# Scores of an attention layer from two fp16 parts instead of two fp32r parts, with the norm weights of queries and keys evened out by a power of two

## The chip, the core and the metric

One core of one Trainium2 chip runs the whole kernel in one launch. The metric is device time in microseconds (us): the median of several executions. A profiled execution of the same program gives the trace; its time is named beside the others, since sums over rows belong to it. The engines are called as in the trace: PE is TensorE, PEld its weight loads, DVE VectorE, ACT ScalarE, POOL GpSimd, SP the engine that issues most DMAs.

## The reference, cut to what matters

An encoder of two layers over 256 positions of width 1024, in fp32. Each layer has a mixer and a channel part. In the mixer 16 heads of width 64 fall into three groups: "a" (4 heads, neighbourhood attention with a bias), "d" (6 heads, dilated windows, partial rotation), "c" (6 query heads on 2 key heads, axial rotation).

```
qa = rms_norm(heads(qa, H_NA), qg[0]);  ka = rms_norm(heads(ka, H_NA), kg[0])
qd = partial_rotary(rms_norm(heads(qd, H_DIL), qg[1]), cos1, sin1)      # kd likewise with kg[1]
qc = axial_rotary(rms_norm(heads(qc, H_GQ), qg[2]), cos_r, sin_r, cos_c, sin_c)   # kc with kg[2]
s = einsum(q, k) * hd ** -0.5 (+ bias or mask);  p = softmax(s);  o = p @ v
x = x + concat(rms_norm of each group's o) @ w_out
```

The norm weights qg and kg have 64 entries for each layer and group; here they are around 4 rather than 1. A score depends on the product of the query's and the key's weights alone, so one number may be moved from the one to the other. The channel part is `x + (gelu(conv(h @ w_g)) * (h @ w_u)) @ w_dn` with 2816 columns in each half.

## The kernel before

All large products are made of two parts for each operand, a high part and the rest, in three matmuls (high by high, high by rest, rest by high). For projections, output projection and the down projection the parts are fp32r; ACT casts the weights from the loaded tile `raw` to `hi`, and DVE subtracts to get `lo` (`split`, lines 638 and 639). Later steps of the channel part use fp16 parts, and so do the products of softmax and values (`weigh`, lines 1204 to 1225). The scores (`scores`, lines 1167 to 1188) use fp32r parts of queries and keys.

The 16 heads of a layer are worked in 8 pairs. For a pair, `scores` issues one burst of 12 matmuls: two query tiles of 128, three products, two heads. The two heads of a pair lie in partitions 0 to 63 and 64 to 127, so each matmul has 64 rows of weights by 128 columns (the queries) and moves 256 columns (the keys). `weigh` issues a burst of 12 as well, with 128 rows by 64 columns of weights (the values) and 256 moved columns of fp16 (the softmax). Between bursts PE is given pieces of the projections and of the output projection (`Weave`), so that it has work while DVE, ACT and POOL do softmax.

Queries and keys are made in `normed` (squares on ACT into a scratch tile of the tag `s2k`, sums, `rstd_of` on POOL with a power of -1/2, then the scaling of the projection into `z`), then in `rotated` (DVE, with tables made by POOL from the norm weights in `tables_d` and `tables_c`), then transposed by PE, and in `transposed` (lines 985 to 994) ACT copies the high part out of PSUM and DVE subtracts to get the rest. For group "a" there is no rotation: `tables_a` multiplies both norm weights into one tile `gna` of 64 columns, and `prep_a` multiplies the query half of `z` by it. In layer 0 the tables are made when the norm weights `gq` and `gk` have landed (they are issued on SP behind the first weights); those of layer 1 are made in the channel part of layer 0.

Nothing is written in its final order. Each call is recorded with a cost in ns (`cost`, lines 396 to 432; `together` gives a burst one cost for all), and `order` (lines 322 to 386) picks again and again the operation that can start first by these costs; at equal times the one that comes first in the program (`rank`). Each engine then works its queue strictly in that order. Tiles of one tag are handed out strictly in program order: an operation whose tile is not next in turn can't be picked (line 352, in which `s.given` is the number handed out so far):

```
                        if t.turn != s.given + n or len(s.free) <= n:
                            at = None
                            break
```

So a change of costs or of the operations that take a tag's tiles can change the order on every engine.

Of the kernel before, what the change touches and what calls it, by code (L numbers as in the profile page):

```python
# [11 lines left out]
F32 = mybir.dt.float32  # L12
F32R = mybir.dt.float32r
F16 = mybir.dt.float16
BF16 = mybir.dt.bfloat16
I32 = mybir.dt.int32
AF = mybir.ActivationFunctionType
ALU = mybir.AluOpType
AX = mybir.AxisListType

P = 128
S = 256
# [3 lines left out]
HD = 64  # L26
H_NA, H_DIL, H_GQ, H_GKV = 4, 6, 6, 2
# [4 lines left out]
DEPTH = 2  # L32
# [8 lines left out]
NS2K = 5  # L41
# [4 lines left out]
LIFT, TOP, TINY = 2.0**-30, 0x7F800000, 1e-30  # L46
# [181 lines left out]
class Plan:  # L228
# [5 lines left out]
    def pool(self, real, name, bufs, space=bass.MemoryType.SB):  # L234
        return PlanPool(self, real, name, bufs, space)
# [200 lines left out]
def encoder_kernel(  # L436
# [21 lines left out]
    nc = Plan(tc)  # L458
# [3 lines left out]
    const = pool("const", 1)  # L462
    wp = pool("wp", 3)
    act = pool("act", 2)
    small = pool("small", 4)
# [4 lines left out]
    def bcast_rows(row, n):  # L470
        return bass.AP(tensor=row.tensor, offset=row.offset, ap=[[0, P], [1, n]])
# [16 lines left out]
    def gains_T(i, n):  # L488
        w = 16 * n
        ps = psw.tile([P, 512], F32, tag="w", name=f"gps{i}")  # L490
        nc.tensor.transpose(ps[:, :w], gl0 if i == 0 else gl1, ident[:w, :w])
        for a in range(n):
            o, v = gains[:, i + a].rearrange("p l k -> p (l k)"), ps[:, 16 * a : 16 * a + 16]
            if i + a == 1:
                nc.vector.tensor_copy(o, v)
            else:
                nc.vector.tensor_scalar_mul(o, v, D**0.5)
# [287 lines left out]

    norms, tables, copied = {}, {}, {}

    def tables_d(l, which):
        g = norms[which]
        cd = act.tile([P, NT, HD], F32, tag=f"cd{which}", name=f"cd{which}{l}", bufs=1)  # L790
        sd = act.tile([P, NT, 16], F32, tag=f"sd{which}", name=f"sd{which}{l}", bufs=1)
        b = lambda v: v.unsqueeze(1).to_broadcast([P, NT, v.shape[1]])
        rot = norms["rot"]
        nc.gpsimd.tensor_tensor(cd, rot[:, :, 0:64], b(g[:, l, 1]), op=ALU.mult)
        for i in range(2):
            o, n = (8 * i, 8 * (1 - i)), 8
            nc.gpsimd.tensor_tensor(
                sd[:, :, o[0] : o[0] + n],
                rot[:, :, 64 + o[0] : 64 + o[0] + n],
                b(g[:, l, 1, o[1] : o[1] + n]),  # L800
                op=ALU.mult,
            )
        tables["d" + which, l] = cd, sd
# [16 lines left out]
        tables["c" + which, l] = cc, sc  # L820

    def tables_a(l):
        gna = act.tile([P, HD], F32, tag="gna", name=f"gna{l}", bufs=1)
        nc.gpsimd.tensor_tensor(gna, norms["q"][:, l, 0], norms["k"][:, l, 0], op=ALU.mult)
        tables["a", l] = gna

    load(0)
    for l in range(DEPTH):
# [79 lines left out]
        if l == 0:  # L908
            gains_T(1, 2)
            rot = const.tile([P, NT, 208], F32, tag="rot", name="rot")  # L910
            nc.sync.dma_start(rot, c_rot.rearrange("(t p) c -> p t c", p=P))
            gq = const.tile([P, DEPTH * 3 * HD], F32, tag="gq", name="gq")
            nc.sync.dma_start(gq, bcast_rows(q_norm_g, DEPTH * 3 * HD))
            gk = const.tile([P, DEPTH * 3 * HD], F32, tag="gk", name="gk")
            nc.sync.dma_start(gk, bcast_rows(k_norm_g, DEPTH * 3 * HD))
            dil = const.tile([P, NT, S], F32, tag="dil", name="dil")
            na_mask = const.tile([P, GRID_W], F32, tag="na", name="na_mask")
            na_repeat(0)
            norms["rot"] = rot
            norms["q"] = gq.rearrange("p (l a d) -> p l a d", l=DEPTH, d=HD)  # L920
            norms["k"] = gk.rearrange("p (l a d) -> p l a d", l=DEPTH, d=HD)

# [62 lines left out]
        def transposed(srcs, both, t, name):  # L985

            n = len(srcs)
            ps = psw.tile([P, 512], F32, tag="w", name=f"tr_{name}")
            for i, src in enumerate(srcs):
                nc.tensor.transpose(ps[:, i * P : (i + 1) * P], src, ident)  # L990
            pv = ps[:, : n * P].rearrange("p (k q) -> p k q", q=P)
            h, o = (z[:, :, t * P : (t + 1) * P] for z in both)
            nc.scalar.copy(h, pv)
            nc.vector.tensor_tensor(o, pv, h.bitcast(F32), op=ALU.subtract)

        def paired(which, group, n, zs, first=0):

            c = which + ("c" if group == "c" else "o")
            both = [act.tile([P, 3, S], F32R, tag=f"{c}{i}", name=f"{which}{i}{group}{l}", bufs=1)[:, :n] for i in range(2)]
            for t in range(NT):  # L1000
                transposed(pairs(zs[t], first, n), both, t, f"{which}{group}{l}{t}")
            return both
# [142 lines left out]
        def prep_a():  # L1145
            if l == 0:
                with nc.behind(hold["prep"]):
                    tables_a(l)
            gna = tables["a", l]
            for t in range(NT):  # L1150
                nm = f"a{l}{t}"
                z = normed(pj["aqk"][t], 2 * H_NA, t, nm)
                nc.vector.tensor_tensor(
                    z[:, 0:4], z[:, 0:4], gna.unsqueeze(1).to_broadcast([P, 4, HD]), op=ALU.mult
                )
                hold["a", t] = z

# [9 lines left out]
        def scores(i):  # L1167

            two = heads[i : i + 2]
            group = two[0].group  # L1170
            qs, ks = turned[group + "q"], turned[group + "k"]
            sps = [psw.tile([P, NT, S], F32, tag="w", name=f"s_{h.name}") for h in two]
            with nc.together(910):
                for t in range(NT):
                    c = slice(t * P, (t + 1) * P)
                    for n, (x, y) in enumerate(((0, 0), (0, 1), (1, 0))):
                        for h, rows_, sp in zip(two, (LOW, HIGH), sps):
                            nc.tensor.matmul(
                                sp[:, t], qs[x][rows_, h.h // 2, c], ks[y][rows_, h.kv if group == "c" else h.h // 2],
                                start=n == 0, stop=n == 2,  # L1180
                            )
            rs = small.tile([P, 2, NT], F32, tag="rs", name=f"rs_{two[0].name}")
            for a, (h, sp) in enumerate(zip(two, sps)):
                h.softens(sp, rs[:, a])
            nc.vector.reciprocal(rs, rs)
            wide = hold["rs", i] = act.tile([P, NT, 2, HD], F32, tag="re", name=f"re_{two[0].name}", bufs=2)
            for t in range(NT):
                nc.gpsimd.tensor_copy(wide[:, t], rs[:, :, t : t + 1].to_broadcast([P, 2, HD]))
# [367 lines left out]
```

## Time and profile before

| | us |
|---|---|
| median of 3 runs | 607.07 (606.72 to 607.68) |
| the profiled execution's own time | 610.95 |
| its span, first to last instruction | 609.2 |
| PE busy in it | 597.3 |
| DVE busy | 489.7 |
| ACT busy | 469.3 |
| POOL busy | 127.2 |
| mean granted clock of TensorE | 0.997 of full |

Busy is the time in which at least one instruction of the engine was under way. PE's matmuls are pipelined and their ends are modelled, so what a matmul costs is read from the distance of one start to the next. All lines of the kernel show as L393, the line that emits them; tiles tell them apart: `psw_w<-act_ko,act_qo` and `psw_w<-act_kc,act_qc` are scores, `psw_w<-act_ph,const_v` and `act_pl,const_v` are `weigh`, `wp_hi` and `wp_lo` are the parts of the weights.

### The profile page before, as it was taken

What the parts mean: (1) busy time and instruction counts of PE and PEld (TensorE: products, weight loads), DVE (VectorE), ACT (ScalarE), POOL (GpSimd) and SP (SyncE); (2) the same over time, 40 slices, a digit from 0 to 9 for tenths busy, and PEclk for the clock granted to TensorE, in tenths of its full rate; (3) what the DMA queues carried; (4) which work ended last, traced back from release to release, by engine and by line L of the source; (5) the groups of instructions that cost most, each with busy time, mean ns of one, the idle gap of its engine ahead of it and who ended that gap; (6) DMA issues with size and microseconds to landing.
All of it is one profiled execution on the core that took longest, in us unless ns stands there. A gap on an engine that the chain in (4) does not pass through costs nothing.

```text
span 609.2 us, 11253 instructions
## 1 busy us (share of the span) xinstructions
PE 597.3 (98%) x4092; PEld 509.0 (84%) x4092; DVE 489.7 (80%) x1095; ACT 469.3 (77%) x1060; POOL 127.2 (21%) x184
## 2 busy tenths in 40 slices
PE   9989999999999999999999999999999999999997
PEld 7879787788887888888889988877888888888886
DVE  5678999989996677867666899998899767777683
ACT  7677879697987778886378979887889897778750
POOL 0543242220021111341014223331101111111100
PEclk9989999999999999999999999999999999999999
DMA  8777222465576946565517721225655766656301
GB/s 292 227 228 216 95 88 80 145 226 190 164 209 221 265 148 220 187 207 190 156 52 225 253 90 69 76 80 200 208 185 178 260 208 208 207 186 211 125 33 70
DMA packets 85260, 104.75 MB, mean 172 GB/s; under 512 B 13044, under 2 KB 73044, under 8 KB 85204
## 3 DMA queue, kind: packets, MB, share of 16 engines
q1 hardware_dynamic: 84100, 103.31, 52.4%
q10 hardware_dynamic: 1104, 0.72, 0.4%
q8 instruction: 32, 0.52, 0.3%
q14 instruction: 24, 0.20, 0.1%
HBM read 102.98 MB, written 1.49 MB: 171 GB/s over the span
## 4 chain that ended last, share of the span: by engine, by line
PE 60%; DVE 16%; ACT 13%; DMA 4%; issue 3%; POOL 3%; ACTq 0%; DVEq 0%; POOLq 0%; SPq 0%
PE psa_a L393 31%; PE psw_w L393 28%; DVE wp_lo L393 5%; DVE act_s2k L393 4%; ACT wp_hi L393 3%; DVE wp_nl L393 3%; ACT act_s2k L393 3%; DMA wp_raw<-in_w_gate_up_dram 3%; ACT act_sw L393 3%; ACT wp_nh L393 2%; DMA wp_raw<-in_w_down_dram 2%; ACT act_hT L393 1%; POOL small_rstd L393 1%; POOL small_pw L393 1%; DVE act_cl L393 1%
## 5 line engine op out<-in xcount | busy, mean ns | idle before, releaser
L393 DVE TENSOR_TENSOR wp_lo<-wp_raw,wp_hi 128x512 fp32r<-128x512 f32 (+2 forms) x220 | 160.3, 756 | 18.3 <-ACT wp_hi L393 17.7
L393 PE MATMUL psw_w<-act_z,wp_nh 128*128 128x256 f16 x1024 | 169.3, 273 | 0.0
L393 ACT CAST wp_hi<-wp_raw 128x512 fp32r<-128x512 f32 (+2 forms) x220 | 138.3, 685 | 18.4 <-DMA wp_raw<-in_w_down_dram 8.6
L393 PE MATMUL psw_w<-act_z,wp_nl 128*128 128x256 f16 x512 | 139.3, 273 | 1.7 <-DVE wp_nl L393 1.6
L393 PE MATMUL psa_a<-wp_hi,act_hT 128*128 128x384 f32 (+2 forms) x448 | 116.2, 338 | 1.7 <-ACT wp_hi L393 1.6
L393 PEld LDWEIGHTS <-wp_nh 128*128 128x128 f16 x1024 | 98.1, 98 | 14.3 <-issue 1.7
L393 DVE SCALAR_TENSOR_TENSOR wp_nl<-wp_raw,small_pw,wp_nh 128x1024 f16<-128x1024 f32 x64 | 81.8, 1282 | 27.6 <-PE psw_w L393 21.0
L393 POOL TENSOR_TENSOR small_pw<-small_m,const_mh 128x1 f32<-128x1 f32 x40 | 41.6, 1042 | 275.9 <-DVE small_m L393 234.2
L393 ACT ACTIVATE wp_nh<-wp_raw,small_pw 128x1024 f16<-128x1024 f32 x64 | 71.4, 1141 | 17.1 <-DVE small_pw L393 13.2
L393 PEld LDWEIGHTS psa_a<-wp_hi,act_hT 128*128 128x128 f32 x448 | 79.1, 191 | 5.5 <-ACT wp_hi L393 2.2
L393 PE MATMUL psa_a<-wp_lo,act_hT 128*128 128x384 f32 (+2 forms) x224 | 76.1, 340 | 2.1 <-DVE wp_lo L393 1.9
L393 ACT ACTIVATE act_sw<-wp_raw 128x1024 f16<-128x1024 f32 x64 | 67.2, 1051 | 7.6 <-DMA wp_raw<-in_w_gate_up_dram 6.8
L393 PE MATMUL psa_a<-wp_hi,act_ch 128*128 128x512 f32 (+1 forms) x176 | 70.5, 402 | 0.5 <-ACT act_ch L393 0.5
L393 PE MATMUL psa_a<-wp_lo,act_ch 128*128 128x512 f32 (+1 forms) x176 | 69.3, 395 | 0.0
L393 PE MATMUL psa_a<-wp_hi,act_cl 128*128 128x512 f32 (+1 forms) x176 | 69.1, 394 | 0.1
L393 PE MATMUL psw_w<-act_hT,wp_hi 128*128 128x512 f32 x192 | 67.7, 396 | 0.0
L393 PEld LDWEIGHTS <-wp_nl 128*128 128x128 f16 x512 | 50.1, 98 | 9.3 <-DVE wp_nl L393 3.6
L393 PE MATMUL psw_w<-act_hT,wp_lo 128*128 128x256 f32 x192 | 53.5, 282 | 0.2 <-DVE wp_lo L393 0.2
L393 PEld LDWEIGHTS psa_a<-wp_lo,act_hT 128*128 128x128 f32 x224 | 42.8, 191 | 5.2 <-DVE wp_lo L393 3.9
L393 PEld LDWEIGHTS psw_w<-act_hT,wp_hi 128*128 128x128 f32 x192 | 35.9, 188 | 7.8
L393 PEld LDWEIGHTS psa_a<-wp_hi,act_ch 128*128 128x128 f32 x176 | 33.2, 189 | 8.1 <-ACT act_ch L393 1.0
L393 PEld LDWEIGHTS psa_a<-wp_hi,act_cl 128*128 128x128 f32 x176 | 33.2, 188 | 8.1 <-DVE act_cl L393 0.5
(154 smaller groups left out, 1013.4 us busy)
## 6 DMA issues: line engine op xcount, KB each, us to landing
wp_raw<-in_w_gate_up_dram SPq DMA_DIRECT2D x44, 1024.0 KB, 5.0
wp_raw<-in_w_down_dram SPq DMA_DIRECT2D x22, 1024.0 KB, 5.5
wp_raw<-in_w_in_dram SPq DMA_DIRECT2D x14, 768.0 KB, 8.2
wp_raw<-in_w_in_dram SPq DMA_DIRECT2D x8, 1024.0 KB, 7.0
wp_raw<-in_w_out_dram SPq DMA_DIRECT2D x8, 768.0 KB, 4.2
wp_raw<-in_w_out_dram SPq DMA_DIRECT2D x4, 512.0 KB, 3.4
act_nab<-dram_scr SPq DMA_DIRECT2D x4, 448.0 KB
wp_raw<-in_w_in_dram SPq DMA_DIRECT2D x4, 192.0 KB, 5.0
```

The lines of the kernel that those rows point to most:

```text
L393: getattr(engine.real, method)(*map(real, args), **{k: real(v) for k, v in kw.items()})
```

## The change

Queries and keys are kept as fp16 parts. So that they fit fp16's range, a new function `balanced` moves a power of two from the keys' norm weights to the queries' or back, for each layer and group, once at the start of layer 0; for group "a" the queries and keys are each multiplied by their own norm weights rather than the queries by both. The cost that the planner is given for a burst of scores goes from 910 to 780. The three products, their number and their shapes stay.

```
+    def balanced(gq, gk):
+        n = 3 * DEPTH
+        sums = []
+        for g, name in ((gk, "k"), (gq, "q")):
+            sq = act.tile([P, n * HD], F32, tag="s2k", name=f"g2{name}", bufs=NS2K)
+            nc.gpsimd.tensor_tensor(sq, g, g, op=ALU.mult)
+            ss = small.tile([P, n], F32, tag=f"gs{name}", name=f"gs{name}", bufs=1)
+            nc.vector.reduce_sum(ss, sq.rearrange("p (a d) -> p a d", d=HD), axis=AX.X)
+            nc.vector.tensor_scalar(ss, ss, TINY, None, ALU.max)
+            sums.append(ss)
+        up, down = sums
+        nc.vector.reciprocal(down, down)
+        nc.vector.tensor_tensor(up, up, down, op=ALU.mult)
+        quarter = const.tile([P, n], F32, tag="quarter", name="quarter")
+        nc.gpsimd.memset(quarter, 0.25)
+        nc.gpsimd.tensor_tensor(up, up, quarter, op=ALU.pow)
+        nc.vector.tensor_scalar(up.bitcast(I32), up.bitcast(I32), TOP, None, ALU.bitwise_and)
+        nc.vector.reciprocal(down, up)
+        for g, s in ((gq, up), (gk, down)):
+            gv = g.rearrange("p (a d) -> p a d", d=HD)
+            nc.gpsimd.tensor_tensor(gv, gv, s.unsqueeze(2).to_broadcast([P, n, HD]), op=ALU.mult)
...
     def tables_a(l):
-        gna = act.tile([P, HD], F32, tag="gna", name=f"gna{l}", bufs=1)
-        nc.gpsimd.tensor_tensor(gna, norms["q"][:, l, 0], norms["k"][:, l, 0], op=ALU.mult)
+        gna = act.tile([P, 2, HD], F32, tag="gna", name=f"gna{l}", bufs=1)
+        for i, which in enumerate("qk"):
+            nc.gpsimd.tensor_copy(gna[:, i], norms[which][:, l, 0])
...
             norms["rot"] = rot
+            balanced(gq, gk)
             norms["q"] = gq.rearrange("p (l a d) -> p l a d", l=DEPTH, d=HD)
...
             nc.scalar.copy(h, pv)
-            nc.vector.tensor_tensor(o, pv, h.bitcast(F32), op=ALU.subtract)
+            nc.vector.tensor_tensor(o, pv, h, op=ALU.subtract)
...
-            both = [act.tile([P, 3, S], F32R, tag=f"{c}{i}", name=f"{which}{i}{group}{l}", bufs=1)[:, :n] for i in range(2)]
+            both = [act.tile([P, 3, S], F16, tag=f"{c}{i}", name=f"{which}{i}{group}{l}", bufs=1)[:, :n] for i in range(2)]
...
                 z = normed(pj["aqk"][t], 2 * H_NA, t, nm)
+                zz = z.rearrange("p (a h) d -> p a h d", a=2)
                 nc.vector.tensor_tensor(
-                    z[:, 0:4], z[:, 0:4], gna.unsqueeze(1).to_broadcast([P, 4, HD]), op=ALU.mult
+                    zz, zz, gna.unsqueeze(2).to_broadcast([P, 2, H_NA, HD]), op=ALU.mult
                 )
...
-            with nc.together(910):
+            with nc.together(780):
```

## Rows read from the trace of the kernel before

**Rows 1.** The page: busy time and share of each engine.
```profile
PE 597.3 (98%) x4092; PEld 509.0 (84%) x4092; DVE 489.7 (80%) x1095; ACT 469.3 (77%) x1060; POOL 127.2 (21%) x184
```
**Rows 2.** Busy time by stage: window, its length, each engine, granted clock, DMA.
```profile
22.00:27.00 5.00, 4.02 (x21) 3.30 (x20) 2.32 (x7) 0.38 (x1) 1.77 (x4) 1.00 0.92 334
27.00:33.00 6.00, 5.68 (x33) 5.21 (x33) 2.69 (x6) 5.03 (x32) 1.99 (x2) 1.00 0.66 198
33.00:36.00 3.00, 0.81 (x4) 0.23 (x2) 2.49 (x8) 2.83 (x12) 2.27 (x3) 1.00 0.86 279
36.00:40.00 4.00, 3.89 (x13) 3.63 (x14) 3.89 (x11) 3.42 (x13) 1.84 (x5) 0.57 0.44 94
50.00:118.00 68.00, 68.00 (x524) 55.68 (x523) 65.25 (x183) 55.81 (x168) 23.20 (x44) 1.00 0.35 108
348.00:414.00 66.00, 65.77 (x515) 54.49 (x513) 61.95 (x180) 54.21 (x167) 21.61 (x38) 1.00 0.30 97
```
**Rows 3.** Timeline of PE around 78 us: start, length, instructions.
```profile
77.24 0.30 PE L393 MATMUL psw_w<-act_ph,const_v 128*64 128x256 f16 x2
...
78.02 0.98 PE L393 MATMUL psw_w<-act_kc,act_qc 64*128 64x256 f32 x12
78.92 0.39 PE L393 MATMUL psa_a<-wp_lo,act_hT 128*128 128x256 f32 x1
```
**Rows 4.** Timeline of PE around 251 us, in the channel part.
```profile
250.89 0.39 PE L393 MATMUL psw_w<-act_z,wp_nh 128*128 128x256 f16 x2
...
251.88 0.38 PE L393 MATMUL psw_w<-act_z,wp_nh 128*128 128x256 f16 x2
```
**Rows 5.** Groups of DVE by form: count, busy us, mean ns.
```profile
L393 DVE RECIPROCAL small_rs<-small_rs 128x4 f32<-128x4 f32 x16 | 2.7, 171 | 0.3 <-ACT act_s2k L393 0.2
L393 DVE TENSOR_TENSOR act_z<-psa_a,small_rstd 128x512 f32<-128x512 f32 x4 | 2.7, 684 | 0.0
L393 DVE TENSOR_REDUCE small_ss<-act_s2k 128x8 f32<-128x512 f32 x4 | 2.7, 669 | 0.0
L393 DVE SCALAR_TENSOR_TENSOR const_v<-psa_a,small_rv,const_v 128x384 f16<-128x384 f32 x4 | 2.3, 610 | 0.0
...
L393 DVE TENSOR_TENSOR act_qo<-psw_w,act_qo 128x384 fp32r<-128x384 f32 x4 | 2.1, 552 | 0.0
...
L393 DVE TENSOR_TENSOR act_z<-act_z,act_gna 128x256 f32<-128x256 f32 x4 | 1.9, 473 | 0.0
```
**Rows 6.** Timeline of POOL in the start of layer 0.
```profile
19.45 0.46 POOL L393 TENSOR_TENSOR act_cdq<-const_rot,const_gq 128x128 f32<-128x128 f32 x1
19.87 0.40 POOL L393 TENSOR_TENSOR act_sdq<-const_rot,const_gq 128x16 f32<-128x16 f32 x2
...
29.70 0.27 POOL L393 TENSOR_SCALAR small_ms<-small_ss,small_he 128x6 f32<-128x6 f32 x1 [5.92 <-ACT act_s2k L393]
```
**Rows 7.** Timeline of DVE in the start of layer 0.
```profile
20.18 0.34 DVE L393 TENSOR_TENSOR act_sw<-act_z,act_sdq 128x48 f32<-128x48 f32 x2
20.44 0.55 DVE L393 TENSOR_TENSOR wp_lo<-wp_raw,wp_hi 128x384 fp32r<-128x384 f32 x1
```
**Rows 8.** The chain that ended last, 30 to 36 us: start, length, what.
```profile
30.06 1.72 POOL small_rstd L393
...
31.80 1.34 ACT act_z L393 x6
...
33.23 0.21 DVE act_sw L393
...
35.59 0.48 DVE wp_lo L393
```
**Rows 9.** Timeline of PE, the two waits at 34.76 and 36.11 us.
```profile
34.76 0.44 PE L393 MATMUL psa_a<-wp_hi,act_hT 128*128 128x384 f32 x1 [1.39 <-ACT wp_hi L393]
36.11 0.44 PE L393 MATMUL psa_a<-wp_lo,act_hT 128*128 128x384 f32 x1 [0.91 <-DVE wp_lo L393]
```
**Rows 10.** Instructions on the tile act_cdq: ns least/median/most, first and last start.
```profile
L393 POOL TENSOR_TENSOR act_cdq<-const_rot,const_gq x2: 460/983/1506, 19.5 to 243.5; 128x128 f32<-128x128 f32 x2
```

## The prediction, made before the change was run

> **What bounds the kernel now.** I read the page's table of engines first, then busy time by stage, then the timelines of PE, POOL and DVE where the change adds work, and the chain of waits there. PE is busy for 98% of the span [rows 1], and in the two stages in which scores are made (50 to 118 us in layer 0, 348 to 414 us in layer 1) it is busy for 68.00 of 68.00 us and 65.77 of 66.00 us [rows 2]. So time taken from PE there should come off the end, unless another engine then sets the pace. The one that could is DVE: 65.25 us of 68.00 and 61.95 of 66.00 in the same stages [rows 2]; what is left to it is 2.75 and 4.05 us.
>
> The start of layer 0 is another matter. From 22 to 36 us PE is busy for 4.02 + 5.68 + 0.81 = 10.5 of 14 us [rows 2]. Two of its waits there are long: 1.39 us for a cast of weights by ACT (PE goes on at 34.76) and 0.91 us for a subtraction by DVE (on at 36.11) [rows 9]. The chain of waits says why: POOL makes the norm of the keys of group "d" (30.06), ACT scales them (31.80), DVE rotates them (33.23), and only behind that, in DVE's queue, stands the subtraction for which PE waits (35.59) [rows 8]. [...] `balanced` runs in this very stretch.
>
> **Shorter bursts of scores.** A burst of scores before takes 78.92 - 78.02 = 0.90 us from its first start to the next work's first start. A burst of `weigh`, also 12 matmuls of 256 columns in pairs, but with fp16 operands, takes 78.02 - 77.24 = 0.78 us [rows 3]. The difference is 0.12 us; there are 8 bursts in each of 2 layers, so 16 x 0.12 = 1.9 us. The bounds: fp16 matmuls of 256 columns in the channel part follow each other at 0.99 / 9 = 0.11 us (nine from 250.89 to 251.88) [rows 4]; six pairs at that distance are 0.66 us, a gain of at most 16 x 0.24 = 3.8 us. Below it nothing, if the pairing of row halves and not the type sets the 0.90. I take the 1.9 of the burst that is nearest in form.
>
> **Group "a".** The multiplication by `gna` covers 512 columns rather than 256: 0.473 us becomes 0.684, that of a 128x512 multiplication [rows 5]. Four of them (two tiles, two layers) add 0.8 us to DVE. PE gets 8 x 0.12 = 1.0 us shorter in each stage and DVE 0.4 longer, so DVE's 2.75 us of room in layer 0 become 1.4: it still fits, but DVE can't always be supplied, and I count half, +0.4 us (0 to 0.8). The two copies of `tables_a` in place of one small multiplication lie on POOL, which is busy for 23.20 of 68 us there [rows 2]: nothing.
>
> **fp16 parts.** ACT and DVE write 24 pairs of tiles as fp16 rather than fp32r. Width and PSUM source stay. The fp16 output that the trace has on DVE, 128x384 for the values, takes 0.610 us against 0.552 for the query's [rows 5], but it also scales. Bounds 0 and 24 x 0.058 = 1.4 us of DVE; I take 0, from the row of the same operation. No DMA is added or moved; no queue of SP changes.
>
> **`balanced`.** On POOL: four multiplications of 384 columns. 128x128 takes 0.46 us and 128x16 some 0.20 [rows 6], so 2.3 ns for each further column and about 1.0 to 1.1 us for 384, in all 4.2; the power on six columns is 1.7 us [rows 8]. Sum 5.9 us. The work that hides it is POOL's own idle time of 5.92 us before 29.70 [rows 6]: it just fits, with nothing to spare. On DVE: two sums of at most 0.67 us and six small operations of 0.17 [rows 5], 2.4 us, against (5.00 - 2.32) + (6.00 - 2.69) = 6.0 us in which DVE idles from 22 to 33 us [rows 2]. I count 0 for both; what it costs if POOL's cover is gone is a rival below.
>
> The wait that it adds: the tables of group "d" now follow a chain of two squares (2.1), a sum, three small operations (1.2), the power (1.7), a mask (0.2) and a multiplication (1.1), some 6 us. The first rotation of queries waits for the table, at 20.18 before, and behind it on DVE stand subtractions of weights (20.44) [rows 7] for which PE waits. The planner knows these costs and can put the subtractions first.
>
> **Order at the start.** `balanced` takes two tiles of the tag `s2k` ahead of the scratch tiles of the queries' squares. Tiles are handed out in program order (line 352), so these squares on ACT can't be picked before POOL's two squares are, and those wait for `gk` to land. ACT's casts of weights need no such tile and go ahead. An earlier cast gains nothing at once: in 22 to 27 us the DMA engines are busy for 0.92 of the time [rows 2], the next weights aren't there. But POOL's queue is then some 6 us longer in the planner's account, so the keys' norm is due later, and ACT's scaling and DVE's rotation of the keys fall behind the casts and subtractions of weights that had to wait for them. The chain of [rows 8] would be cut. I take it that the 1.39 us for ACT's cast goes and the 0.91 us for DVE stays, since DVE now has the queries' rotation to do later too: -1.4 us. Bounds: 0 (another wait instead), and -(1.39 + 0.91 + 1.7) = -4.0 us, if the low clock goes with both waits.
>
> **Sum.** -1.9 + 0.4 + 0 + 0 - 1.4 = -2.9 us. The profiled execution took 610.95 us, 609.2 of it span and 1.75 around; it would take 608.05. It is 3.9 us above the median of the runs, 607.07; the terms are stretches of engine work and go over as they are: 604.2 us.
>
> **Rivals.** *The scores alone.* The start is re-ordered, but its waits only move, since the weights come when the DMA brings them. Then -1.9 + 0.4 = -1.5: 605.6 us. For it: the DMA share of 0.92. Against it: the weights for which PE waited at 34.76 are held up by ACT's queue, not by a transfer [rows 8, 9].
>
> *DVE takes PE's place.* It is busy for 96% and 94% of the stages of the scores [rows 2]. If the order leaves it no slack, a PE that is 1.9 us faster waits 1.9 us more for subtractions: no change, 607.1 us. That the bursts don't get shorter at all ends close to it (-1.4 + 0.4: 606.1). Against it: PE hardly waits in these stages, and DVE's room after the change is still 1.4 us.
>
> *POOL comes late* (slower). The same 128x128 multiplication took 0.46 us in the start and 1.51 us at 243.5 us, beside a busy DVE [rows 10]. If each of the four multiplications is stretched by that 1.05 us, POOL has 4.2 us more than its cover; the keys' norm at 30.06, the scaling, the rotation and the subtraction behind them all come 4 us later, and PE with them: -1.9 + 0.4 + 4.2 = +2.7, 609.8 us. It decides from 2.7 us of lateness on. Against it: in the start itself the row is 0.46. [...]
>
> **How the numbers follow.** My forecast has a chance of 0.45, the scores alone 0.25, DVE in PE's place (or bursts as long as before) 0.17, POOL late 0.13. About 0.2%, 1.2 us, is what a measurement of this kernel can tell from no change. The forecast's cases are faster by more than that; the scores alone end at 1.5 us, close to it, so 0.15 of its 0.25 count as faster and 0.10 as the same. Faster 0.60, same 0.10 + 0.17 = 0.27, slower 0.13. The range goes down to the forecast with the whole start term, -1.9 + 0.4 - 4.0 = -5.5, 601.6 us, and up past DVE's case to 607.5 us; it leaves out POOL's case and some 0.05 below.
>
> **What would show it.** Scores: distance from a burst's first start to the next work's near 0.78 us, in all 16. Group "a": 0.68 us on DVE for `act_z<-act_z,act_gna`, and no new PE wait for `wp_lo` in the stages of the scores. `balanced`: multiplications of about 1.1 us on POOL, and the keys' norm no later than 30 us. The order: ACT's casts ahead of its scaling of the keys, PE's 1.39 us gone. The prediction is wrong if bursts stay at 0.90 us, if PE waits for DVE between 50 and 118 us, or if POOL's multiplications take well over 1.1 us and PE's wait near 35 us grows.

## The result and the profile after

The changed kernel takes 615.0 us (median of 4 runs, 613.1 to 615.8), the kernel before beside it 606.9 us: a ratio of 1.0113, interval 1.0084 to 1.0141. It is slower by 8 us where 3 us less were forecast. The profiled execution has a span of 613.0 us against 609.2.

The page's table of engines, after (before: [rows 1]):
```profile
PE 597.3 (97%) x4092; PEld 504.2 (82%) x4092; DVE 494.7 (81%) x1103; ACT 468.5 (76%) x1060; POOL 132.8 (22%) x192
```
PE is busy for the same 597.3 us although its bursts got shorter; this column also holds modelled ends, so distances between starts say more. Busy time by stage, after, with the columns of [rows 2]:
```profile
27.00:33.00 6.00, 4.49 (x28) 4.17 (x27) 4.42 (x12) 4.14 (x29) 5.82 (x11) 1.00 1.04 322
33.00:36.00 3.00, 3.00 (x21) 2.88 (x20) 2.15 (x9) 2.21 (x8) 2.82 (x4) 1.00 0.86 218
36.00:40.00 4.00, 3.64 (x20) 3.21 (x19) 3.88 (x10) 3.96 (x15) 1.93 (x6) 1.00 0.88 232
50.00:118.00 68.00, 65.54 (x505) 51.95 (x504) 65.10 (x181) 53.51 (x157) 22.25 (x43) 1.00 0.37 103
348.00:414.00 66.00, 64.73 (x518) 52.37 (x517) 62.04 (x180) 55.80 (x179) 21.36 (x38) 1.00 0.29 95
```
Two things are to be seen. In the start, PE works in 33 to 36 us, where it stood still for 2.2 us before, and the clock of 36 to 40 us is 1.00 instead of 0.57; on the other hand it idles for 1.51 us in 27 to 33 us. In the stage of layer 0's scores PE, which was busy for all of its 68.00 us, now idles for 2.46 us, while DVE is as busy as before (65.10 against 65.25).

The timeline of PE around 84 us, after; the last field is what a wait was for (before: [rows 3]):
```profile
83.37 0.83 PE L393 MATMUL psw_w<-act_kc,act_qc 64*128 64x256 f16 x12
84.12 0.66 PE L393 MATMUL psw_w<-const_ident,act_s2k 128*128 128x128 f32 x4
...
86.50 0.50 PE L393 MATMUL psa_a<-wp_hi,act_mixT_hi 128*128 128x512 f32 x1 [1.72 <-DVE act_z L393]
```
The burst takes 84.12 - 83.37 = 0.75 us. But behind it and four transposes PE waits 1.72 us for DVE, where the kernel before had no such wait.

DVE's groups by form, after (before: [rows 5]), and POOL in the start of layer 0 (before: [rows 6]):
```profile
L393 DVE TENSOR_TENSOR act_z<-act_z,act_gna 128x512 f32<-128x512 f32 x4 | 2.7, 676 | 0.0
...
L393 DVE TENSOR_TENSOR act_qo<-psw_w,act_qo 128x384 f16<-128x384 f32 x4 | 2.1, 548 | 0.0
...
L393 DVE TENSOR_REDUCE small_gsk<-act_s2k 128x6 f32<-128x384 f32 x1 | 0.5, 541 | 0.0
```
```profile
19.83 0.92 POOL L393 TENSOR_TENSOR act_s2k<-const_gk 128x384 f32<-128x384 f32 x1 [0.27 <-DMA const_gk<-in_k_norm_g_dram]
20.72 1.14 POOL L393 TENSOR_TENSOR act_s2k<-const_gq 128x384 f32<-128x384 f32 x1
...
28.09 0.83 POOL L393 TENSOR_TENSOR const_gq<-const_gq,small_gsk 128x384 f32<-128x384 f32 x1
28.88 1.14 POOL L393 TENSOR_TENSOR const_gk<-const_gk,small_gsq 128x384 f32<-128x384 f32 x1
29.99 0.46 POOL L393 TENSOR_TENSOR act_cdq<-const_rot,const_gq 128x128 f32<-128x128 f32 x1
...
32.69 1.50 POOL L393 TENSOR_TENSOR small_rstd<-small_ms,const_mh 128x6 f32<-128x6 f32 x1
```
The operations cost what the prediction gave them: 0.68, 0.55 and 0.54 us on DVE, 0.83 to 1.14 us for a multiplication of 384 columns on POOL. The keys' norm comes at 32.69 instead of 30.06 [rows 8], and the table of group "d" at 29.99 instead of 19.45 [rows 6]. The waits of PE that stand where those of [rows 9] stood, with the row of DVE on which the first of them hangs:
```profile
30.66 0.63 DVE L393 TENSOR_TENSOR act_sw<-act_z,act_sdq 128x48 f32<-128x48 f32 x2 [1.33 <-POOL act_sdq L393]
...
32.60 0.55 PE L393 MATMUL psw_w<-const_ident,act_z 128*128 128x128 f32 x3 [1.51 <-DVE act_z L393]
...
39.57 0.44 PE L393 MATMUL psa_a<-wp_lo,act_hT 128*128 128x384 f32 x1 [0.36 <-DVE wp_lo L393]
```
In all 1.87 us of waiting for 2.30, and no low clock behind it. The 1.51 us come from POOL: DVE's rotation of the queries waits 1.33 us for the table that POOL makes behind `balanced`. The first burst of scores starts at 48.57 us, before at 50.49. So in this execution the changed kernel is 1.9 us ahead at 50 us, and 3.8 us behind at the end.

A second profile of the same kernel (`g1_changed_again`, below) is only 0.25 us ahead there. Its window of 27 to 33 us, with a granted clock of 0.72, a wait in it for a cast of weights by ACT, and its first burst:
```profile
27.00:33.00 6.00, 4.67 (x16) 4.09 (x17) 4.81 (x11) 5.39 (x32) 4.12 (x7) 0.72 0.72 192
```
```profile
28.18 0.44 PE L393 MATMUL psa_a<-wp_hi,act_hT 128*128 128x384 f32 x1 [1.36 <-ACT wp_hi L393]
...
50.24 0.83 PE L393 MATMUL psw_w<-act_ko,act_qo 64*128 64x256 f16 x12
```
What both profiles share is the part behind it: from the first burst to the last instruction the kernel before takes 609.2 - 50.49 = 558.7 us, the changed one 613.0 - 48.57 = 564.4 and 616.1 - 50.24 = 565.9. What went wrong lies behind the start.

### The profile page after: what moved, and what is told of

Its sections match the earlier page's. It is cut to its first block, busy times and chain, and to the rows that moved or that the text cites. A ratio compares the mean times of both kernels' runs of the same rounds, so it can differ in the third digit from the quotient of the medians.

```text
span 613.0 us, 11297 instructions
## 1 busy us (share of the span) xinstructions
PE 597.3 (97%) x4092; PEld 504.2 (82%) x4092; DVE 494.7 (81%) x1103; ACT 468.5 (76%) x1060; POOL 132.8 (22%) x192
## 3 DMA queue, kind: packets, MB, share of 16 engines
q1 hardware_dynamic: 84100, 103.31, 53.6%
HBM read 102.98 MB, written 1.49 MB: 170 GB/s over the span
## 4 chain that ended last, share of the span: by engine, by line
PE 66%; DVE 12%; ACT 10%; DMA 6%; POOL 4%; issue 3%; ACTq 0%; POOLq 0%; DVEq 0%
PE psw_w L393 35%; PE psa_a L393 31%; DVE act_s2k L393 3%; DVE wp_lo L393 3%; DMA wp_raw<-in_w_gate_up_dram 2%; ACT wp_hi L393 2%; ACT act_s2k L393 2%; DVE wp_nl L393 2%; POOL small_pw L393 1%; DMA wp_raw<-in_w_down_dram 1%; ACT act_sw L393 1%; ACT wp_nh L393 1%; DMA wp_raw<-in_w_in_dram 1%; POOL small_rstd L393 1%; DVE act_z L393 1%
## 5 line engine op out<-in xcount | busy, mean ns | idle before, releaser
L393 DVE TENSOR_TENSOR wp_lo<-wp_raw,wp_hi 128x512 fp32r<-128x512 f32 (+2 forms) x220 | 162.1, 762 | 16.2 <-ACT wp_hi L393 15.9
L393 POOL TENSOR_TENSOR small_pw<-small_m,const_mh 128x1 f32<-128x1 f32 x40 | 43.7, 1093 | 276.8 <-DVE small_m L393 240.0
```

The source lines that it names most:

```text
L393: getattr(engine.real, method)(*map(real, args), **{k: real(v) for k, v in kw.items()})
```

## The experiments

All ratios are to the kernel before on the same chip, with their 95% intervals; the kernel before had medians between 609.1 and 610.0 us there.

### The parts one by one

Theory 1 was that the planner's new order costs the time, theory 2 that fp16 gains nothing or costs elsewhere, theory 3 that the evening-out at the start costs it. *fp16 parts alone*, with 910 kept; the order of every queue is then that of the kernel before:
```diff
-            nc.vector.tensor_tensor(o, pv, h.bitcast(F32), op=ALU.subtract)
+            nc.vector.tensor_tensor(o, pv, h, op=ALU.subtract)
...
-            both = [act.tile([P, 3, S], F32R, tag=f"{c}{i}", ...
+            both = [act.tile([P, 3, S], F16, tag=f"{c}{i}", ...
```


> The kernel before with fp16 queries and keys alone: no evening out of the norm weights, group a and the burst's cost of 910 as before, so every engine's queue stands in the order of before. Theory 1 (the loss of the whole change comes from the order that the planner makes anew when costs and tiles change): the bursts fall from 0.908 to 0.759 us, as in the changed kernel, and all of it reaches the end: 16 x 0.149 = 2.4 us less than before. Theory 2 (fp16 itself costs elsewhere, in ACT's and DVE's copies or in PE's clock): no gain, or slower by a part of the 8 us. Theory 3 (the work of evening out at the start costs the 8 us): 2.4 us less here too.

Measured: 1.0015 (0.9988 to 1.0042). PE's 16 bursts take 0.76 us instead of 0.91 by their starts, 2.3 us in the sum; nothing of it is seen at the end.

*The same with 780:*
```diff
-            with nc.together(910):
+            with nc.together(780):
```


> As the first, with the burst's cost of 780 that the planner is given: the same work, another order. Theory 1: it leaves the 2.4 us less of the first run, by 1 to 4 us to either side, with new waits of PE for DVE that the first doesn't have. Theory 3: within 0.5 us of the first, 2.4 us less than before.

Measured: 1.003 (1.000 to 1.006); by these intervals it can't be told from the same with 910. PE's wait of 1.72 us for DVE's `act_z` is in its trace, ending at 85.64 us, as are waits of 0.64 and 0.35 us that end at 169.21 and 173.60 us.

*The evening-out alone* (`balanced` and its call added to the kernel before, nothing else):

> The kernel before with the evening out of the norm weights alone (fp32r scores, group a and cost as before). Theory 3: slower than before by about 8 + 2.4 = 10 us, most of it lost before the first burst of scores. Theory 1: slower by a part of it only, 2 to 6 us, and not at the start but where PE waits for DVE later, because the order behind the start is another.

Measured: 1.0047 (1.0024 to 1.0071). The orders of the queues differ from before only between 15 and 47 us, and its first burst of scores starts at 50.48 us, before at 50.49. The loss comes later; PE's longest waits there are for weights and for what stands behind them, in 207 to 229 us.

*Group "a" alone* (two factors in `gna`, 512 columns):

> The kernel before with both norm weights of group a multiplied each into its own half (512 columns on DVE rather than 256, two small copies on POOL). The forecast's 0.4 us more, at most 0.8, if DVE's extra 0.8 us is what counts; theory 1: 1 to 4 us to either side, since four operations have another cost for the planner; theory 3: within 0.8 us of before.

Measured: 0.9998 (0.997 to 1.0026). It costs nothing.

The parts thus leave the evening-out with 0.5%, and not where it works. In all these traces PE also waits for weights in layer 0's channel part, 160 to 230 us, behind the transfers of layer 1's bias.

### Without the transfers of layer 1's bias

```diff
-            2: [na_repeat], 4: [na_diagonals], 6: [na_bias_mask],
+            2: [lambda n: nabs.update({n: nabs[0]})],
```


> The kernel before, with layer 1 using the neighbourhood bias table that layer 0 built: the four small bias transfers, the two that spread them and the mask step, which the kernel before runs among layer 0's channel part, are left out (layer 1's own bias is not applied). Theory A (in layer 0's channel part, about 160 to 230 us, the weights arrive behind those transfers, and PE's waits there, 2 to 5 us in each profile and none of the kind in layer 1, set the pace): 2 to 5 us below the kernel before. Theory B (those waits are chance of one execution and what matters is the order that the planner gave each queue): within 1 us of the kernel before.

> The fp16 parts alone, 910 ns kept, without layer 1's bias transfers (left out as in the kernel beside it); every queue in the same order as that kernel's. PE's bursts are 2.4 us shorter in the sum. Theory A: what the fp16 parts gain was swallowed in the transfer-paced channel part, so 1.2 to 2.4 us below the kernel without the transfers. Theory B (VectorE, ScalarE and GpSimd pace the score stages themselves, so that the gain is gone before the channel part begins): at most 0.7 us below it.

> The evening-out of the norm weights alone, without layer 1's bias transfers (left out). Theory A (the 3 us that it cost were waits for weights behind the transfers): within 1 us of the kernel without both. Theory B (the chain of squares, power, masks and products at the start, and the order there, cost the 3 us): 2 to 4 us above it.

> The whole change without layer 1's bias transfers (left out). If the 8 us of the whole change came from waits behind those transfers (theory A), at most 1 us above the kernel before without them, and perhaps 1 to 2 us below. If they came from the start and from the order of the queues (theory B), 5 to 8 us above it.

Measured: 0.9967 (0.994 to 0.9993), 0.9966 (0.9945 to 0.9987), 0.9988 (0.9971 to 1.0004) and 1.0032 (1.0012 to 1.0052). The transfers cost some 0.3%, but they swallow no gain: fp16 is level with its partner without them too, and the whole change stays 0.65% above it. For the fp16 parts theory A of these runs falls. For the evening-out it does not fall whole: without the transfers it costs 0.21%, which can't be told from nothing, where it cost 0.47% with them, and the whole change 0.65% where it cost 1.1%. The section on the tile of 24 bytes comes back to this.

The two kernels of one order show where the fp16 gain goes. From the timeline of PE, the first burst of layer 0 and a matmul of the output projection behind the last one, without fp16 parts:
```profile
50.65 0.98 PE L393 MATMUL psw_w<-act_ko,act_qo 64*128 64x256 f32 x12
...
110.69 0.50 PE L393 MATMUL psa_a<-wp_hi,act_mixT_lo 128*128 128x512 f32 x1
```
and with them:
```profile
48.66 0.83 PE L393 MATMUL psw_w<-act_ko,act_qo 64*128 64x256 f16 x12
...
87.38 0.50 PE L393 MATMUL psa_a<-wp_hi,act_mixT_hi 128*128 128x512 f32 x1 [0.17 <-DVE act_z L393]
...
108.44 0.50 PE L393 MATMUL psa_a<-wp_hi,act_mixT_lo 128*128 128x512 f32 x1
```
The stage takes 60.04 us without and 59.78 us with them. Eight bursts gave 8 x 0.149 = 1.19 us; 0.26 us is left in this pair of profiles. The rest goes back in pieces of 0.05 to 0.17 us at matmuls that wait for DVE (`act_z`, `const_x`, `act_mixT_lo`, and the row at 87.38).

### The order, and where the evening-out stands

The changed kernel again, and the whole change with 910:

> The changed kernel as it is, on the same chip as the runs beside it. If the parts measured one by one add up (fp16 parts 0 to +1, the 780 ns order +1 to +2, evening-out +2 to +3, the two factors of group a 0), it lies 4 to 6 us above the kernel before. If the parts make each other worse, 7 us or more.

> The whole change with the planner told 910 ns for a burst, as before, instead of 780 ns; nothing else differs. Theory 1 (the order that 780 ns gives brings PE's waits at 84 us, 1.7 us for VectorE's scaling of group a, and at 166 to 173 us, 1.5 us for VectorE's weight rests): 1.5 to 3 us below the changed kernel, which leaves the cost of the evening-out, 2 to 3 us above the kernel before. Rival (those waits come from the evening-out or from group a's factors): within 0.7 us of the changed kernel.

Measured: 1.0109 (1.0085 to 1.0133) and 1.0048 (1.0026 to 1.0071), medians 616.8 and 611.6 us. The one number that is told to the planner is worth 0.6%, 3.7 us by the ratios and 5.2 by the medians, and it is the truer number, nearer to the 0.76 us that a burst takes, that gives the slower kernel. DVE's timeline in the changed kernel shows how:
```profile
83.96 0.68 DVE L393 TENSOR_TENSOR wp_lo<-wp_raw,wp_hi 128x512 fp32r<-128x512 f32 x1
84.56 1.28 DVE L393 TENSOR_REDUCE small_nm<-psw_w 128x2 f32<-128x512 f32 x2
85.76 1.51 DVE L393 TENSOR_TENSOR act_z<-psa_a,small_rstd 128x512 f32<-128x512 f32 x2
```
The two scalings of group "a" (`act_z<-psa_a`), which empty the tiles `psa_a` that PE's next output projection writes, stand behind a weight subtraction and both maxima; PE waits from 84.8 to 86.5. With 910 (here the last kernel below, the orders are the same) DVE does one scaling first, and PE goes on without a stop:
```profile
83.84 0.69 DVE L393 TENSOR_TENSOR act_z<-psa_a,small_rstd 128x512 f32<-128x512 f32 x1
84.45 0.68 DVE L393 TENSOR_TENSOR wp_lo<-wp_raw,wp_hi 128x512 fp32r<-128x512 f32 x1
85.05 1.28 DVE L393 TENSOR_REDUCE small_nm<-psw_w 128x2 f32<-128x512 f32 x2
```
```profile
84.53 0.66 PE L393 MATMUL psw_w<-const_ident,act_s2k 128*128 128x128 f32 x4
84.95 0.48 PE L393 MATMUL psa_a<-wp_hi,act_mixT_hi 128*128 128x512 f32 x1
```
The order of 780 has more such waits, in the profiles of both runs of the changed kernel: 0.73 us for `wp_lo` behind 107 us, and those that begin the channel part:
```profile
169.23 0.38 PE L393 MATMUL psw_w<-act_hT,wp_lo 128*128 128x256 f32 x1 [0.63 <-DVE wp_lo L393]
...
173.62 0.18 PE L393 MATMUL psw_w<-small_qb,const_warm 128*128 128x1 bf16 x1 [0.35 <-DVE small_qb L393]
```
1.72 + 0.73 + 0.63 + 0.35 = 3.4 us, none of which the kernels with 910 have at these places. That this is close to 3.7 us proves little: fp16 alone with 780 has all four of these waits (1.72, 0.27, 0.64 and 0.35 us), and there 780 costs only 0.15%, which can't be told from nothing. The lengths of the two stages say more, since they differ less from one execution to the next than the whole does. From the first burst of a layer to its last matmul on `act_mixT_lo` PE takes, in us, over all profiles of a kind:

| | layer 0 | layer 1 |
|---|---|---|
| fp32r parts, 910 (10 profiles) | 73.95 to 74.43 | 73.53 to 73.65 |
| fp16 parts, 910 (5) | 73.71 to 74.20 | 73.12 to 73.33 |
| the whole change, 780 (4) | 76.49 to 78.02 | 74.17 to 74.20 |
| fp16 parts alone, 780 (1) | 77.52 | 72.63 |

With 780 the stage of layer 0 is longer by more than 2 us in every profile; a part of that it may have gained ahead of the first burst, which the table doesn't show. In layer 1 it costs the whole change 0.8 to 1.1 us, while fp16 alone gains 0.5 to 0.6 us by it there. So it is not one order that costs, but what the planner makes of this number together with the rest.

The evening-out for layer 1 alone, moved into layer 0's channel part (layer 0 keeps its norm weights; the excerpt compares with the kernel that has the evening-out alone):
```diff
-            balanced(gq, gk)
...
-            7: [await_gate, lambda n: tables_d(n, "q"), ...
+            7: [await_gate, balanced, lambda n: tables_d(n, "q"), ...
```


> The kernel before with the evening-out for layer 1 alone, run in layer 0's channel part just ahead of layer 1's rotation tables; layer 0 keeps its own gains, so every queue's order is that of the kernel before up to about 225 us. Theory 3 (the 2 to 3 us are paid at the start, where the table of the first group and its rotation stand behind the chain): within 0.8 us of the kernel before. [...]

Measured: 1.0053 (1.0029 to 1.0078). Theory 3 falls: with the start untouched the cost is as large. But most of it can't be the operations either: PE's extra waits, for weights and behind them in 187 to 228 us, come before they run (from 245 us on).

The bias transfers of layer 1 moved later, in the kernel before:
```diff
-            2: [na_repeat], 4: [na_diagonals], 6: [na_bias_mask],
+            6: [na_repeat],
...
+            10: [na_bias_mask],
```


> The kernel before with the transfers and the mask of layer 1's bias moved four steps of the channel part later (steps 6, 8 and 10 where 2, 4 and 6 stood), to where the transfer engines are idle by the page; everything is computed. If weights wait behind these transfers between 160 and 230 us, as the runs without them say (2.1 us), 1.5 to 2.5 us below the kernel before; if the waits only move with them, no change.

Measured: 0.999 (0.9972 to 1.0008). No change that can be told, although in its trace PE's waits for weights between 160 and 230 us are gone and only one of 0.75 us, at 260.13 us, stands behind them.

### A tile of 24 bytes

What all kernels with the evening-out have in common is a new tile, `quarter`, of 24 bytes in each partition (12 where it serves layer 1 alone; that kernel is counted with the 24 below). It lies in the pool `const`, which is opened ahead of the pools of the weights and of the activations:
```
    const = pool("const", 1)
    wp = pool("wp", 3)
    act = pool("act", 2)
    small = pool("small", 4)
```
By this order the tiles that weights are transferred into lie further on by what `quarter` takes, and so do all activation tiles behind them. That is the author's reckoning from the program: the trace shows no addresses, and how many bytes the tiles move, which grid they lie on and whether 24 bytes are rounded up no run shows. A pad of that size in the kernel before, which nobody reads:
```diff
+            pad = const.tile([P, 6], F32, tag="pad", name="pad")
+            nc.gpsimd.memset(pad, 0.25)
```


> The kernel before with one more constant tile of 24 bytes per partition, filled once by GpSimd and read by nobody; every other instruction and every queue's order is as before. By the sizes of the tiles, 32-byte slots as the allocator counts them, all weight and activation tiles then lie 32 bytes further on, off the 64-byte grid on which the kernel before has them. Layout theory (the evening-out costs what it does because its small constant tile shifts the tiles that the weights are transferred into, and transfers into shifted tiles take longer): 2 to 3 us above the kernel before, with the packets of the main queue taking 2 to 4% more time for the same bytes. Chain theory (the operations of the evening-out cost it): within 0.5 us of the kernel before.

The evening-out and the whole change with that tile made 64 bytes long:
```diff
-        quarter = const.tile([P, n], F32, tag="quarter", name="quarter")
+        quarter = const.tile([P, 16], F32, tag="quarter", name="quarter")[:, :n]
```


> The evening-out alone, as in the kernel with only that, but with its constant tile made 64 bytes long instead of 24, so that the tiles behind it stay on the 64-byte grid; instructions and orders are the same as there. Layout theory: within 0.8 us of the kernel before, packets as short as in the kernel before. Chain theory: 2 to 3 us above it.

> The whole change with that constant tile 64 bytes long. Layout theory: 2 to 3 us below the changed kernel, so 4.5 to 6 us above the kernel before, what is left being the 780 ns order. Chain theory: 7 to 8 us above the kernel before, like the changed kernel.

> The whole change with that constant tile 64 bytes long and 910 ns for a burst. Layout theory: both costs gone, within 1 us of the kernel before, perhaps 1 us below it (PE's bursts are 2.4 us shorter). Chain theory: 2.5 us above it, like the change with 910 ns alone.

Measured: the pad 1.0051 (1.0024 to 1.0077); with 64 bytes the evening-out 1.0049 (1.0024 to 1.0073), the whole change 1.0096 (1.0061 to 1.0131) and the whole change with 910 1.0028 (1.0004 to 1.0052). The unread tile costs as much as the evening-out. The layout theory was wrong about 64 bytes: they do not mend it. So it was mended to a coarser grid, and two last runs tested that: the pad with 256 bytes, and the change with `quarter` in the pool `small`, behind all others:
```diff
-            pad = const.tile([P, 6], F32, tag="pad", name="pad")
+            pad = const.tile([P, 64], F32, tag="pad", name="pad")
```
```diff
-        quarter = const.tile([P, n], F32, tag="quarter", name="quarter")
+        quarter = small.tile([P, n], F32, tag="quarter", name="quarter", bufs=1)
...
-            with nc.together(780):
+            with nc.together(910):
```


> The kernel before with the same unread constant tile, now 256 bytes long, of which the same 24 are filled; the same instructions in the same order as with the 24-byte pad. Layout theory as mended (what counts is where the tiles behind it lie on a grid coarser than 64 bytes; moved by 256 bytes they lie on a 256-byte grid as in the kernel before): within 0.8 us of the kernel before, with packets as short as there. Rival (not the place: one more instruction, or a program that was built anew, costs the 2.7 us): 2 to 3 us above it, packets long.

> The whole change with 910 ns for a burst and the evening-out's small constant put into the pool of small tiles, which lies behind all others, so that the weight and activation tiles lie exactly where the kernel before has them; the same instructions and orders as the change with 910 ns. Layout theory as mended: within 1 us of the kernel before, packets as short as there. Rival (the operations of the evening-out cost it): 2 to 3 us above the kernel before.

Measured: 1.0004 (0.9977 to 1.0032) and 0.9993 (0.997 to 1.0016). Both costs are gone. The intervals of the two pads still overlap a little; but of the kernels with 910 and the bias transfers in their old place the six that are shifted by 24 or 64 bytes lie at 1.0028 to 1.0053, and the four that aren't, or by 256, at 0.9993 to 1.0015. From each page, the span and the main DMA queue (packets, MB, share of 16 engines), first the kernel before, then the pad of 24 and the pad of 256 bytes:
```profile
span 609.2 us, 11253 instructions
...
q1 hardware_dynamic: 84100, 103.31, 52.4%
```
```profile
span 612.1 us, 11254 instructions
...
q1 hardware_dynamic: 84100, 103.31, 54.8%
```
```profile
span 610.1 us, 11254 instructions
...
q1 hardware_dynamic: 84100, 103.31, 52.6%
```
For the same packets and bytes the engines are busy for 319, 335 and 321 us of their time (share by span): 5% longer with 24 bytes, not with 256. Over all profiles the gap is smaller and clear: 329 to 336 us in the nine shifted kernels that transfer the bias, 319 to 324 us in the six others that do so in its old place (328 us with the bias moved later).

The packets themselves show it without overlap. The trace keeps the size and the time of each. Of the packets of 1024 bytes, 50432 in each profile and most of them weights, 3.0 to 3.3% took over 46 ns in each of the nine profiles without a shift or with 256 bytes, and 20 to 25% in each of the eleven with a shift of 24 or 64. The packets of 256 bytes, nearly all of which bring the neighbourhood bias into `act_nab` (four transfers of 448 KB), have a median of 18 ns in all of the nine and of 29 to 33 ns in all of the eleven. So the shift acts on the bias too, and there most: this fits the smaller cost without the transfers of layer 1's bias. The stages of the scores are as long with it as without, 73.95 to 74.08 us in layer 0 for the kernels with fp32r parts and the bias, so in these stages at least the engines don't work more slowly on shifted tiles.

One place shows the later weights in a row, the timeline of ACT in the channel part, with 24 bytes and then with 256:
```profile
209.91 0.62 ACT L393 CAST act_ch<-act_s2k 128x512 fp32r<-128x512 f32 x1 [2.43 <-DVE act_s2k L393]
211.91 2.00 ACT L393 CAST wp_hi<-wp_raw 128x1024 fp32r<-128x1024 f32 x2 [1.38 <-DMA wp_raw<-in_w_down_dram]
```
```profile
209.91 0.62 ACT L393 CAST act_ch<-act_s2k 128x512 fp32r<-128x512 f32 x1 [2.25 <-DVE act_s2k L393]
210.44 1.99 ACT L393 CAST wp_hi<-wp_raw 128x1024 fp32r<-128x1024 f32 x2
```
Up to the cast of 209.91 both are level; then the weights of the down projection have not landed with 24 bytes, ACT waits 1.38 us, and its queue stays that much later. PE meets it at the next `act_ch`, again 24 and then 256:
```profile
228.22 0.49 PE L393 MATMUL psa_a<-wp_hi,act_ch 128*128 128x512 f32 x1 [1.28 <-ACT act_ch L393]
```
```profile
226.99 0.48 PE L393 MATMUL psa_a<-wp_hi,act_ch 128*128 128x512 f32 x1
```
The change with 910 has this wait too, and with `quarter` in the pool `small` it has not, with the same instructions in the same order on PE:
```profile
230.06 0.49 PE L393 MATMUL psa_a<-wp_hi,act_ch 128*128 128x512 f32 x1 [1.23 <-ACT act_ch L393]
```
```profile
224.25 0.48 PE L393 MATMUL psa_a<-wp_hi,act_ch 128*128 128x512 f32 x1
```
Of the kernels with 910 and the bias transfers in their old place, all six whose weight tiles are shifted by 24 or 64 bytes wait there, for 1.08 to 1.28 us; the five that aren't shifted or by 256 don't. It is a sign of the shift and not its price: the three profiles of shifted kernels with 780 and the bias show no such wait, and the pad of 256 bytes has a wait of 1.41 us at 208.08 us that the pad of 24 bytes has not, so that from the last matmul of layer 0's output projection to the first burst of layer 1 the two take 225.48 and 225.72 us. Where the 0.5% is lost within an execution these profiles don't show.

## Why the prediction was wrong

*What it left out: the order that 780 gives.* The text before the prediction said that "a change of costs" can change every queue, and the prediction worked this out for the start alone. The burst's cost (line 1173) and the turns of the tiles (line 352) together had no term in the sum for the stages behind. That is about half of the loss: +3.7 us by the ratios with and without it (1.0109 to 1.0048). The rows show it as waits of PE for DVE that are in each profile with 780 and in none with 910 (the longest, 1.71 to 1.72 us, in all five). Its size depends on what stands beside it: 0.15% with fp16 alone, which is within the noise, 0.7% with the 64-byte tile.

*`balanced`, "I count 0 for both".* For the end time its operations held to this: POOL's multiplications took 0.83 to 1.14 us where 1.05 was said, and moving them or leaving all but the tile out changes nothing that can be told. The cover was not what was said: from the first square (19.83) to the table of group "d" (29.99) are 10.2 us where "some 6" were reckoned, since POOL makes the norms of the queries in between (1.33 us at 22.50, 1.49 us at 26.63). What costs the other 3.4 us (1.0048 to 0.9993) is `quarter` and the shift behind it, which no step thought of. That "no DMA is added or moved" was true of the queue and not of the addresses.

*Shorter bursts of scores.* The bursts got shorter by more than was said, 2.4 us against 1.9. The step that failed is the one before it, "time taken from PE there should come off the end, unless another engine then sets the pace". The rival *DVE takes PE's place* describes it: of 1.19 us in layer 0, 0.26 us came through in the pair of profiles, and fp16 alone ends at 1.0015. The sign that the prediction named for being wrong, PE waiting for DVE between 50 and 118 us, is there: 0.17 us at 87.38 with fp16 parts alone, 1.72 us in the changed kernel. Against that rival stood that PE hardly waited there and that DVE had 2.75 us of room; room as an average over a stage was no room at the places where PE needed a result.

*Order at the start.* In the first profile PE reached its first burst 1.9 us earlier, against 1.4 us forecast. That was luck: in the second, of the same kernel, PE waits 1.36 us for a cast by ACT after all, the clock is 0.72 in 27 to 33 us, and the first burst starts at 50.24, 0.25 us earlier than before; with the evening-out alone it starts at 50.48. The term of -1.4 us is not borne out. The rival *The scores alone*, that the waits only move, describes these two profiles as well as the forecast describes the first. The 1.7 us in the lower bound of this term is an estimate, (1 - 0.57) x 4.0 us by the clock of 36 to 40 us in [rows 2]; no run shows it as a time. What the traces show is that there, before, three matmuls of 384 columns take 0.96 us from start to start (37.32 to 38.28), and after, at a clock of 1.00, 0.52 us (36.50 to 37.02).

*Group "a" and fp16 parts.* 0.676 and 0.548 us; with 0.9998 for the first alone, nothing to add.

*POOL comes late* was right that the keys' norm comes later, by 2.6 us, and PE's wait of 1.51 us does hang on POOL, by the queries' table; but all waits there are together no longer than before (1.87 us for 2.30). Its four multiplications took 0.83 to 1.14 us, near the 1.05 reckoned without any stretch; none took the 1.05 us more that the rival gave to each. (The 1.51 us of [rows 10], at 243.52, lay beside a subtraction on DVE from 243.49 to 244.71.) DVE's subtractions took longer, beside POOL's two squares (19.83 to 21.86 us) and then behind them:
```profile
19.99 1.18 DVE L393 TENSOR_TENSOR wp_lo<-wp_raw,wp_hi 128x384 fp32r<-128x384 f32 x1
...
22.66 0.54 DVE L393 TENSOR_TENSOR wp_lo<-wp_raw,wp_hi 128x384 fp32r<-128x384 f32 x1
```
Two took 1.18 us there; the other 30 of this form before 60 us took 0.51 to 0.62. The rows show that the longer ones stand beside POOL's squares, not what makes them longer. By these times it is 1.3 us of DVE in the start and, with the evening-out alone at 50.48 us, PE nothing that can be told.

The sum by what was measured: 0 for the fp16 parts, 0 for group "a", 0 for the start (0.01 us with the evening-out alone), +3.7 for the order, +3.4 for the place of the tile, 7.1 us; the changed kernel is 6.6 us slower by its ratio of 1.0109 and 7.7 by the medians. That this comes out is no check, since the last two terms are two steps of one chain of ratios (1.0109, 1.0048, 0.9993). Taken in the other order they could part otherwise: the change with 780 and `quarter` in the pool `small` was not run. Open is also how much of the order's share belongs to which single wait, and what in the transfer makes a shifted tile slower: 128 bytes weren't tried, nor a shift of the sources.

No kernel here that does the whole work beats the one before: the change with 910 and `quarter` in the pool `small`, 0.9993 (0.997 to 1.0016), is level with it.

## What to carry to other kernels

A sum over changed operations is complete only when two further things are priced: a cost that a planner reads (try the old number with the new code; the truer one need not give the better order), and where every tile behind a new one comes to lie. Put small constants behind the large transfer targets (0.9993 here), or fill them up (256 bytes 1.0004; 24 and 64 bytes 1.0028 to 1.0053), and when a harmless addition costs time compare the DMA queue's share for the same bytes (here 54.8% for 52.4%). Take a second profile before a gain in the start is put down to a change (1.9 us in the first here, 0.25 us in the second). Time taken from an engine that is busy for 100% of a stage was worth only what the engine at 96% let through (0.26 of 1.19 us in layer 0).

## What the runs showed of the hardware

An unread tile of 24 bytes in front of the tiles that weights are transferred into made the same 84100 packets take 5% more of the DMA engines' time (3% between the means of all shifted and all other profiles with the bias in its old place) and the kernel 0.5% slower (1.0024 to 1.0077); a tile of 256 bytes did neither (0.9977 to 1.0032), and in kernels that add 64 bytes the share was as high as with 24 (54.3% of 611.0 us, 332 us, for the evening-out alone). Packets of 256 bytes went from a median of 18 ns to 29 to 33 ns; of those of 1024 bytes 20 to 25% instead of 3% took over 46 ns. What in a transfer makes the difference, and what a tile of between 64 and 256 bytes does, the runs don't show.

Twelve matmuls of 64 rows by 256 columns in pairs of row halves took 0.759 us in fp16 and 0.908 us in fp32r, the former a little under the 0.78 us of a burst of `weigh` [rows 3].

In the start of the changed kernel a subtraction of 128x384 on DVE (`wp_lo<-wp_raw,wp_hi`) took 1.18 us beside POOL's squares and 0.51 to 0.62 us elsewhere up to 60 us. POOL's multiplication of 128x384 took 0.83 to 1.14 us there: 1.14 us beside those longer subtractions (20.72), and 1.14 us also where DVE was busy for only the first 0.45 us of it (28.88).
